# The shift half of a modulation vector: row products on TensorE replaced by ScalarE multiplications and GpSimd sums

## The chip, the cores and the metric

The kernel runs on one core of a Trainium2 chip. The metric is the device time of one execution in microseconds (us), taken as the median of several runs. The profile is of one further execution on the same kind of chip. In its rows PE is TensorE (matrix products; PEld is its weight load), DVE is VectorE, ACT is ScalarE, POOL is GpSimd, and SP is the engine that here only issues DMAs; a q behind an engine's name means its sequencer.

## The reference, cut to what matters

The program is one block of a hybrid encoder (1024 tokens of width 1024): attention, a state-space branch, a merge and a feed-forward part. What matters here is its beginning.

```python
mod = jax.nn.silu(c) @ w_ada[l] + b_ada[l]                 # c: (1, 1024), w_ada: (1024, 6144)
shift1, scale1, gate1, shift2, scale2, gate2 = jnp.split(mod, 6, axis=-1)
h = rms_norm(x, norm1_w[l]) * (1.0 + scale1) + shift1
proj = h @ w_in[l]
```

All values are float32. `shift1` and `scale1` are vectors of 1024 numbers, each the product of one row vector, silu(c), with a 1024 x 1024 block of `w_ada`. Every further step of the program needs `h`.

## The kernel before, in words

`h` is kept transposed: channels on the 128 partitions, tokens along the free axis, in eight channel tiles k of two token halves each. It is kept as the sum of two tiles of a rounded float32 type, `hh` (high part) and `hl` (low part, the rest), and every weight tile is split the same way into `twh` and `twl`. A product of the two is three TensorE products: high by high, low weight by high, high weight by low.

**The modulation** is made in two halves hf of 512 channels. Half 0 gives what channel tiles 0 to 3 need, half 1 what tiles 4 to 7 need. `mod_load(hf, k)` (line 336) brings a 512 KB tile `wada` with 128 rows of `w_ada` (channels k*128 to k*128+127 of c) and two column blocks of 512: block 0 belongs to the shift, block 1 to the scale. Seven such buffers go round (`WADA = 7`). `mod_step(hf, k, wt)` then does two things, for k = 0 to 7:

- scale: DVE multiplies block 1 by silu(c), one number per partition, and adds it to `macc` (lines 345 and 347). After eight steps `macc` holds 128 partial sums per column, one on each partition.
- shift: TensorE multiplies the 128 x 1 column of silu(c) by block 0 and sums over the eight steps into one row of 512 numbers in PSUM, `psr` (line 348).

`mod_scale(hf)` copies that row to SBUF as `srow` (line 356, ACT), and turns `macc` into a column on the partitions: four products of a 128 x 128 piece of `macc` with a vector of ones, which also add up the 128 partitions (line 359). `mod_shift(hf)` turns the row by four products with a single one (line 366), then DVE adds the bias and the norm weight (`modc`, `s`; lines 159 and 368). From then on, `x_high` (line 323, ACT, writes `hh`), `x_full` (line 327, DVE, writes `xf`) and `x_low` (line 159, DVE, `hl` = `xf` - `hh`) can run for the channel tiles of that half.

**The input tokens**: `x_load` brings 128 tokens of x to one of four `xs` buffers, `x_square` sums their squares (line 301, ACT, with a scratch tile `junk`), `x_scale` applies the root mean square, and `x_turn(half, k)` turns channel tile k of four token tiles with four products into one of two PSUM banks `pst` (line 314). For the first token half, tiles 4 to 7 are turned before their modulation is known, and `x_keep` copies them from PSUM to SBUF as `xT` (line 319, ACT), so that the banks and the `xs` buffers come free.

**The first products** of the projection, `first_mm` (line 380, `psq`), run between these steps.

What sets the order: in this whole stage the instructions of SP, DVE, ACT and PE stand in the order in which the program is written (a manual schedule). Each engine takes its own in that order, and waits at each for what it reads. GpSimd has nothing to do in this stage. The names of the tile buffers matter: a tile with `bufs=2` takes over the buffer of the tile before the last of the same `tag`, and its writer waits until that one's readers are done. Behind half 1's eight steps ACT has two weight casts (`twh`, line 173) and DVE the two differences that go with them (`twl`, line 159); then come `mod_scale(1)` and `mod_shift(1)`. The loads of the second half of x wait for the last `x_turn` of the first half, which frees the `xs` buffers.

Of the kernel before, what the change touches and what calls it, by code (L numbers as in the profile page):

```python
# [9 lines left out]
F32 = mybir.dt.float32  # L10
F32R = mybir.dt.float32r
BF16 = mybir.dt.bfloat16
AF = mybir.ActivationFunctionType
ALU = mybir.AluOpType
# [4 lines left out]
P = 128  # L19
S = 1024  # L20
D = 1024
NT = S // P
KT = D // P
# [68 lines left out]
def block(ctx: ExitStack, tc: tile.TileContext, ia, out, upto=99, dbg=None):  # L92
    nc = tc.nc
    V, A, G, T = nc.vector, nc.scalar, nc.gpsimd, nc.tensor
# [41 lines left out]
    ones = cp.tile([P, P], F32, name="ones")  # L136
# [5 lines left out]
    sc = cp.tile([P, 8], F32, name="sc")  # L142
# [15 lines left out]
    def tt(e, o, a, b, op):  # L158
        e.tensor_tensor(out=o, in0=a, in1=b, op=op)  # L159
# [111 lines left out]
    with tc.tile_pool(name="p0", bufs=1) as p0, tc.tile_pool(name="ps0", bufs=1, space=PSUM) as ps0:  # L271
# [8 lines left out]
        ps = ps0.tile([P, 512], F32, name="psv", tag="psv", bufs=2)  # L280
# [16 lines left out]
            dma(xs[t], x_in[t * P:(t + 1) * P, :])  # L297

        def x_square(t):
            junk = p0.tile([P, D], BF16, name="junk", tag="junk", bufs=1)  # L300
            A.activation(junk, xs[t], AF.Square, accum_out=ss[:, t:t + 1])

        def x_scale(t):
# [29 lines left out]
        accs, psrs, pcs = {}, {}, {}  # L333

        def mod_load(hf, k):
            wt = p0.tile([P, 2, 512], F32, name="wada", tag="wada", bufs=WADA)
            dma(wt, w_ada[k * P:(k + 1) * P, 0:2 * D].rearrange("p (a c) -> p a c", a=2)[:, :, hf * 512:(hf + 1) * 512])
            return wt

        def mod_step(hf, k, wt):  # L340

            if k == 0:
                accs[hf] = p0.tile([P, 512], F32, name="macc", tag="macc", bufs=2)
                psrs[hf] = ps0.tile([P, 512], F32, name="psr", tag="psv", bufs=2)
                V.tensor_scalar(out=accs[hf], in0=wt[:, 1], scalar1=sc[:, 0:1], scalar2=None, op0=ALU.mult)
            else:
                V.scalar_tensor_tensor(out=accs[hf], in0=wt[:, 1], scalar=sc[:, k:k + 1], in1=accs[hf], op0=ALU.mult, op1=ALU.add)
            T.matmul(psrs[hf][0:1], sc[:, k:k + 1], wt[:, 0], start=k == 0, stop=k == KT - 1)

        rows_ = {}  # L350

        def mod_scale(hf):

            cs = slice(4 * hf, 4 * hf + 4)
            rows_[hf] = p0.tile([1, 512], F32, name="srow", tag="srow", bufs=1)
            A.copy(rows_[hf], psrs[hf][0:1])
            pcs[hf] = ps0.tile([P, 512], F32, name="psv", tag="psv", bufs=2)
            for j in range(4):
                T.matmul(pcs[hf][:, j:j + 1], accs[hf][:, j * P:(j + 1) * P], ones[:, 0:1], start=True, stop=True)

        def mod_shift(hf):

            cs = slice(4 * hf, 4 * hf + 4)
            ps = pcs[hf]
            for j in range(4):
                T.matmul(ps[:, 4 + j:5 + j], rows_[hf][0:1, j * P:(j + 1) * P], ones[0:1, 0:1], start=True, stop=True)
            tt(V, modc[:, 1, cs], ps[:, 0:4], vecT[:, BA + 8 + 4 * hf:BA + 12 + 4 * hf], ALU.add)
            V.scalar_tensor_tensor(out=s1[:, cs], in0=modc[:, 1, cs], scalar=1.0, in1=vecT[:, N1 + 4 * hf:N1 + 4 * hf + 4],
                                   op0=ALU.add, op1=ALU.mult)
            tt(V, modc[:, 0, cs], ps[:, 4:8], vecT[:, BA + 4 * hf:BA + 4 * hf + 4], ALU.add)  # L370
# [18 lines left out]
        with tc.manual_schedule(engines={mybir.EngineType.SP, mybir.EngineType.DVE, mybir.EngineType.Activation, mybir.EngineType.PE}):  # L389
            for k in range(KT):  # L390
                wt = mod_load(0, k)
                if k < 4:
                    x_load(k)
                    x_square(k)
                mod_step(0, k, wt)
                if k == 3:
                    turn_rows()
                if k == 5:
                    rstd(p0, rs[:, 0:4], ss[:, 0:4], D, 4)
                    x_scale(1)  # L400
                    x_scale(3)
                if k >= 6:
                    x_scale(2 * (k - 6))
            traws = [tw_raw(qkv_srcs(0, kh)) for kh in range(2)]
            mod_scale(0)
            x_turn(0, 0)
            mod_shift(0)
# [48 lines left out]
            mod_shift(1)  # L456
            first_mm(0, 3, (0, 1, 2))
            x_square(4)
            traws = [tw_raw(qkv_srcs(1, kh)) for kh in range(2)]
            for k in range(4, KT):  # L460
# [963 lines left out]
    with tc.tile_pool(name="p5", bufs=1, reuse_waits="tile") as p5, \  # L1424
# [41 lines left out]
        for n, (i, second) in enumerate(jobs):  # L1466
# [13 lines left out]
            for half in range(2):  # L1480
                ps = part[i][half] if i in part else ps5.tile([P, 512], F32, name="psg", tag="psg", bufs=6)
# [39 lines left out]
    with tc.tile_pool(name="p6", bufs=1, reuse_waits="tile") as p6:  # L1521
# [9 lines left out]
        def turned(hf, k):  # L1531
            ps = ps7.tile([P, 512], F32, name="pst", tag="ps1", bufs=4)
            for j in range(4):
                T.transpose(ps[:, j * P:(j + 1) * P], x1[hf * 4 + j][:, k * P:(k + 1) * P], ident)
            return ps
# [4 lines left out]
        for t in range(NT):  # L1540
# [3 lines left out]
            for n in range(2):  # L1544
# [3 lines left out]
                ps = ps7.tile([P, 512], F32, name="pso", tag="ps2", bufs=4)  # L1548
# [12 lines left out]
            if t == 4:  # L1561
                for k in range(KT):
                    ps = turned(0, k)
# [52 lines left out]
        with tc.manual_schedule(engines={mybir.EngineType.PE, mybir.EngineType.DVE, mybir.EngineType.Activation}):  # L1616
# [4 lines left out]
            for j in range(HK):  # L1621
                for q, f in enumerate((fa, fb)):
                    f[j] = tmp("fab")
                    k = q * HK + j
                    ps = ps7.tile([P, 512], F32, name="pst", tag=("ps1", "ps2")[q], bufs=4)
# [278 lines left out]
    with tc.tile_pool(name="p8", bufs=1, reuse_waits="tile") as p8:  # L1904
# [71 lines left out]
        for h in "01":  # L1976
            pss = [banks(first), banks(1 - first)]
            ops = []
            for q in range(2):
                for k in range(KR):  # L1980
                    ops.append((ahead(n), plain_b[q, k]))
                    n += 1
                    j = len(ops) - 1
# [56 lines left out]
```

## Time and profile before

| | |
|---|---|
| time of the kernel, median of 3 runs | 2457.29 us (2456.69 to 2461.17) |
| time of the profiled execution | 2455.24 us |
| its span, first to last instruction | 2453.4 us |
| TensorE busy | 2387.5 us, 97% of the span |
| VectorE busy | 1706.5 us, 70% |
| ScalarE busy | 1092.0 us, 45% |
| GpSimd busy | 829.2 us, 34% |
| mean granted TensorE clock | 0.993 |

The stage that the change touches begins with the span and lies between about 22 and 58 us of it. In a timeline row the first number is the start in us from the beginning of the span, the second the length in us; then come engine, line, operation, the tile written and the tiles read, their shapes, and how many instructions were merged into the row. What stands in square brackets is the idle time of the engine just before, and what ended it. In a row of the chain of waits (the chain of work that ended last) stand start, length, engine, tile and line. In a row of grouped instructions the numbers behind the bar are the busy time in us and the mean length of one in ns, then the idle time before them.

### The profile page before, as it was taken

To read this page: it belongs to the slowest core of one execution; us is meant where nothing else is said; L and a number is where in the kernel's file an instruction comes from. 1 tells how busy PE (TensorE), PEld (TensorE's weight loads), DVE (VectorE), ACT (ScalarE), POOL (GpSimd) and SP (SyncE) were. 2 spreads that over 40 slices of the span, in tenths; PEclk is the share of its full clock that TensorE was granted. 3 is DMA by queue.
4 is the path that set the end of the run, shared out by engine and by line. 5 is a ranking of instruction groups with operands and counts; after the bars stand their busy time and mean duration, and the time that the engine had idled before them with its cause. 6 is when DMAs were issued, how large, how long until landed. Compare 5 with 4: busy or idle time off the path is not lost.

```text
span 2453.4 us, 32245 instructions
## 1 busy us (share of the span) xinstructions
PE 2387.5 (97%) x11307; PEld 1900.2 (77%) x11307; DVE 1706.5 (70%) x2325; ACT 1092.0 (45%) x1884; POOL 829.2 (34%) x637
## 2 busy tenths in 40 slices
PE   8999999999989999999989999999999999999999
PEld 4998877888867777777767767787787888788887
DVE  5876435777756666666577796558568887767794
ACT  5455413555566666666333343354242222364430
POOL 0221107666611111110356665534006885023200
PEclk9999999999999999999999999999999999999999
DMA  7664751333531212111667765486325554654422
GB/s 257 185 184 139 255 170 65 95 103 111 183 114 52 91 52 80 57 53 48 223 207 222 223 209 177 142 282 202 125 86 193 196 174 159 231 172 142 153 79 83
DMA packets 288596, 366.53 MB, mean 149 GB/s; under 512 B 33962, under 2 KB 168850, under 8 KB 288434
## 3 DMA queue, kind: packets, MB, share of 16 engines
q1 hardware_dynamic: 216246, 288.77, 36.9%
q10 hardware_dynamic: 72187, 75.70, 9.1%
q8 instruction: 90, 1.47, 0.2%
q14 instruction: 73, 0.59, 0.1%
HBM read 250.54 MB, written 113.84 MB: 149 GB/s over the span
## 4 chain that ended last, share of the span: by engine, by line
PE 84%; DVE 7%; DMA 3%; issue 2%; ACT 2%; POOL 0%; ACTq 0%; SPq 0%; DVEq 0%; POOLq 0%
PE pst L1053 5%; PE psg L211 4%; PE psg L213 4%; PE psg L212 4%; PE pp L1503 4%; PE pp L1505 4%; PE pp L1504 4%; PE p L1919 3%; PE p L1918 3%; PE p L1917 3%; PE psc L916 3%; PE psc L917 3%; PE psc L918 3%; PE psq L518 3%; PE psq L519 3%; PE psq L517 3%
## 5 line engine op out<-in xcount | busy, mean ns | idle before, releaser
L1040 DVE TENSOR_REDUCE nm<-pss 128x1 f32<-128x1024 f32 x128 | 156.7, 1225 | 125.2 <-PE pss L1038 122.8
L1042 ACT ACTIVATE pf<-pss,nm 128x1024 f32<-128x1024 f32 x128 | 142.8, 1116 | 98.9 <-PE pst L1053 96.3
L159 DVE TENSOR_TENSOR pl<-pst,ph 128x512 fp32r<-128x512 f32 x256 | 167.6, 683 | 27.1 <-ACT ph L173 27.0
L1053 PEld LDWEIGHTS pst<-masks,pf 128*128 128x128 f32 x1024 | 117.5, 140 | 73.3 <-issue 33.3
L517 PE MATMUL psq<-twh,hh 128*128 128x512 f32 (+1 forms) x448 | 168.3, 380 | 3.0 <-ACT twh L173 3.0
L518 PE MATMUL psq<-twl,hh 128*128 128x512 f32 (+1 forms) x448 | 169.3, 379 | 0.9 <-DVE twl L159 0.9
L173 ACT CAST ph<-pst 128x512 fp32r<-128x512 f32 x256 | 145.7, 585 | 54.9 <-PE pst L1053 38.2
L1053 PE MATMUL pst<-masks,pf 128*128 128x128 f32 x1024 | 157.3, 276 | 13.0 <-DVE pl L159 10.6
L519 PE MATMUL psq<-twh,hl 128*128 128x512 f32 (+1 forms) x448 | 168.6, 377 | 0.0
L159 POOL TENSOR_TENSOR av<-av,rz 64x512 f32<-64x512 f32 x32 | 41.9, 1310 | 348.1 <-issue 99.3
L1917 PE MATMUL p<-o,o 128*128 128x512 f32 x400 | 153.6, 390 | 3.0 <-ACT o L173 1.6
L1918 PE MATMUL p<-o,o 128*128 128x512 f32 x400 | 155.2, 389 | 0.2 <-DVE o L159 0.2
L1919 PE MATMUL p<-o,o 128*128 128x512 f32 x400 | 153.7, 389 | 0.0
L173 ACT CAST wop<-ws 128x512 fp32r<-128x512 f32 x116 | 71.8, 621 | 124.4 <-PE pp L1505 78.7
L862 DVE SCALAR_TENSOR_TENSOR tap<-pad,cwT,tap 128x1024 f32<-128x1024 f32 x96 | 123.4, 1285 | 5.2 <-ACT tap L860 3.8
L159 POOL TENSOR_TENSOR ws<-r,r 128x512 f32<-128x512 f32 x29 | 41.4, 1428 | 220.3 <-DMA r<-in_w_mlp_dram 168.9
L159 POOL TENSOR_TENSOR sl<-sl 128x512 f32<-128x512 f32 x32 | 49.4, 1546 | 179.5 <-DVE o L159 72.4
L173 ACT CAST o<-sl 128x512 fp32r<-128x512 f32 x92 | 56.9, 623 | 104.6 <-PE p L1919 88.7
L1091 PE MATMUL pv<-pl,v 128*64 128x512 f32 x256 | 102.1, 419 | 0.0
L159 DVE TENSOR_TENSOR o<-sl,o 128x512 fp32r<-128x512 f32 x92 | 72.7, 793 | 41.3 <-ACT o L173 41.3
L211 PE MATMUL psg<-hh,whi 128*128 128x512 f32 x224 | 95.7, 427 | 1.2 <-ACT ost L1002 1.2
L517 PEld LDWEIGHTS psq<-twh,hh 128*128 128x128 f32 x448 | 84.5, 189 | 15.0 <-ACT twh L173 3.4
(457 smaller groups left out, 7035.6 us busy)
## 6 DMA issues: line engine op xcount, KB each, us to landing
ar<-r SPq DMA_DIRECT2D x100, 256.0 KB
wada<-in_w_ada_dram SPq DMA_DIRECT2D x48, 512.0 KB
r<-in_w_mlp_dram SPq DMA_DIRECT2D x32, 512.0 KB
sl<-in_w_mlp_dram SPq DMA_DIRECT2D x64, 256.0 KB
r<-in_w_in_dram SPq DMA_DIRECT2D x26, 512.0 KB
r<-ro ACTq DMA_DIRECT2D x49, 256.0 KB
r<-as SPq DMA_DIRECT2D x48, 256.0 KB
xb<-cst ACTq DMA_DIRECT2D x20, 512.0 KB
```

Of the source, the lines that this page charges most:

```text
L159: e.tensor_tensor(out=o, in0=a, in1=b, op=op)
L173: (e_hi or A.copy)(hi, src)
L211: T.matmul(ps, hi[:, k], ahi[k][half], start=k == 0, stop=False)
L517: T.matmul(o, hhi[k][half][:, sl], hi[:, k % 2, :n], start=k == 0, stop=False)
L518: T.matmul(o, hhi[k][half][:, sl], lo[:, k % 2, :n], start=False, stop=False)
L519: T.matmul(o, hlo[k][half][:, sl], hi[:, k % 2, :n], start=False, stop=k == KT - 1)
L1040: V.tensor_reduce(out=nm, in_=ps, axis=AX.X, op=ALU.max, negate=True)
L1042: A.activation(pfs[u], ps, AF.Exp, bias=nm, accum_out=zall[:, u:u + 1])
L1053: T.transpose(pt[:, k], pf[:, (hf * 4 + k) * P:(hf * 4 + k + 1) * P], ident)
L1917: T.matmul(ps, a[:, 0, sl], b[0], start=start, stop=False)
L1918: T.matmul(ps, a[:, 0, sl], b[1], start=False, stop=False)
L1919: T.matmul(ps, a[:, 1, sl], b[0], start=False, stop=stop)
```

## The change

Only half 1 changes. Its shift is made in the way in which the scale is: ACT multiplies block 0 of `wada` by silu(c) (a `Copy` with a scale per partition) into a 128 x 512 tile `sacc`, and GpSimd adds the eight products up, seven sums in all. The result holds 128 partial sums per column, and `mod_shift(1)` turns it and adds up the partitions by four products with the full vector of ones. The eight row products of half 1 (`psr`, line 348), the copy of its row (`srow`) and the four products with a single one are gone. Half 0 stays as it is.

The first product (k = 0) takes a third `macc` buffer and is the tile into which GpSimd adds. The others take the two buffers of the tag `junk`, which had one buffer and is also the scratch tile of `x_square`. So product k + 2 on ACT waits for the sum k on GpSimd, and the first two of `x_square`'s later tiles wait for the last two sums.

```diff
         def x_square(t):
-            junk = p0.tile([P, D], BF16, name="junk", tag="junk", bufs=1)
+            junk = p0.tile([P, D], BF16, name="junk", tag="junk", bufs=2)
             A.activation(junk, xs[t], AF.Square, accum_out=ss[:, t:t + 1])
...
             if k == 0:
-                accs[hf] = p0.tile([P, 512], F32, name="macc", tag="macc", bufs=2)
-                psrs[hf] = ps0.tile([P, 512], F32, name="psr", tag="psv", bufs=2)
+                accs[hf] = p0.tile([P, 512], F32, name="macc", tag="macc", bufs=3)
                 V.tensor_scalar(out=accs[hf], in0=wt[:, 1], scalar1=sc[:, 0:1], scalar2=None, op0=ALU.mult)
             else:
                 V.scalar_tensor_tensor(out=accs[hf], in0=wt[:, 1], scalar=sc[:, k:k + 1], in1=accs[hf], op0=ALU.mult, op1=ALU.add)
-            T.matmul(psrs[hf][0:1], sc[:, k:k + 1], wt[:, 0], start=k == 0, stop=k == KT - 1)
+            if hf:
+                t = p0.tile([P, 512], F32, name="sacc", tag="macc" if k == 0 else "junk", bufs=3 if k == 0 else 2)
+                A.activation(t, wt[:, 0], AF.Copy, scale=sc[:, k:k + 1])
+                if k == 0:
+                    accs[2] = t
+                else:
+                    tt(G, accs[2], accs[2], t, ALU.add)
+            if hf == 0:
+                if k == 0:
+                    psrs[hf] = ps0.tile([P, 512], F32, name="psr", tag="psv", bufs=2)
+                T.matmul(psrs[hf][0:1], sc[:, k:k + 1], wt[:, 0], start=k == 0, stop=k == KT - 1)
...
-            rows_[hf] = p0.tile([1, 512], F32, name="srow", tag="srow", bufs=1)
-            A.copy(rows_[hf], psrs[hf][0:1])
+            if hf == 0:
+                rows_[hf] = p0.tile([1, 512], F32, name="srow", tag="srow", bufs=1)
+                A.copy(rows_[hf], psrs[hf][0:1])
...
             for j in range(4):
-                T.matmul(ps[:, 4 + j:5 + j], rows_[hf][0:1, j * P:(j + 1) * P], ones[0:1, 0:1], start=True, stop=True)
+                js = slice(j * P, (j + 1) * P)
+                if hf == 0:
+                    T.matmul(ps[:, 4 + j:5 + j], rows_[hf][0:1, js], ones[0:1, 0:1], start=True, stop=True)
+                else:
+                    T.matmul(ps[:, 4 + j:5 + j], accs[2][:, js], ones[:, 0:1], start=True, stop=True)
```

On TensorE, the place from the turning of tiles 3 and 4 of x to the turning of half 1's `macc` stands like this before:

```order
L314 MATMUL pst<-masks,xs 128x128 x8
L348 MATMUL psr<-wada,sc 1x512
L380 MATMUL psq<-twh,hh_0_348 128x400 x4
L348 MATMUL psr<-wada,sc 1x512
L314 MATMUL pst<-masks,xs 128x128 x8
L348 MATMUL psr<-wada,sc 1x512
L314 MATMUL pst<-masks,xs 128x128 x4
L348 MATMUL psr<-wada,sc 1x512
L359 MATMUL psv<-ones,macc 128x1 x4
```

and like this with the change, where the last product reads `macc`, which DVE makes:

```order
L314 MATMUL pst<-masks,xs 128x128 x8
L394 MATMUL psq<-twh,hh_0_348 128x400 x4
L314 MATMUL pst<-masks,xs 128x128 x12
L369 MATMUL psv<-ones,macc 128x1 x4
L394 MATMUL psq<-twl,hh_0_348 128x400
```

The four row products of this piece, and the four ahead of it, are gone; nothing else changed its place. On ACT, the same stretch, from the high parts `hh` of tiles 0 to 3 of the first half (numbers 344 to 350) to the casts, before:

```order
L323 ACTIVATE hh_0_344<-pst,modc,s_334 128x512
L323 ACTIVATE hh_0_346<-pst,modc,s_334 128x512
L323 ACTIVATE hh_0_348<-pst,modc,s_334 128x512
L173 CAST twh<-traw 128x2x400
L323 ACTIVATE hh_0_350<-pst,modc,s_334 128x512
L319 COPY xT<-pst 128x512 x4
L173 CAST twh<-traw 128x2x400 x2
L356 COPY srow<-psr 1x512
```

and with the change:

```order
L323 ACTIVATE hh_0_344<-pst,modc,s_334 128x512
L349 ACTIVATE sacc<-wada,sc 128x512
L323 ACTIVATE hh_0_346<-pst,modc,s_334 128x512
L349 ACTIVATE sacc<-wada,sc 128x512 x2
L323 ACTIVATE hh_0_348<-pst,modc,s_334 128x512
L173 CAST twh<-traw 128x2x400
L349 ACTIVATE sacc<-wada,sc 128x512 x2
L323 ACTIVATE hh_0_350<-pst,modc,s_334 128x512
L319 COPY xT<-pst 128x512
L349 ACTIVATE sacc<-wada,sc 128x512
L319 COPY xT<-pst 128x512 x2
L349 ACTIVATE sacc<-wada,sc 128x512
```

The eight products stand between the high parts and the copies of x; the last one (not shown) stands behind the fourth copy and ahead of the two casts. On DVE and SP no instruction is added, removed or moved. GpSimd gets the seven sums as its first work. Outside this stage the order is the same on every engine, but for one product of the later projection by `w_o`, which stands two places further back.

## The prediction

> **What bounds the kernel now.** I read first the page's shares of the chain of waits, then the busy times of the stretch that the change touches, then the chain through that stretch. The page's chain:
>
> ```profile
> PE 84%; DVE 7%; DMA 3%; issue 2%; ACT 2%; POOL 0%; ACTq 0%; SPq 0%; DVEq 0%; POOLq 0%
> ```
>
> TensorE sets the end, so time taken off its order early comes off the end, unless another engine is late there. The stretch from 26 to 48 us (length; busy us of PE, PEld, DVE, ACT and POOL, each with its count; clock; DMA share; GB/s):
>
> ```profile
> 26.00:48.00 22.00, 21.64 (x100) 12.83 (x101) 15.53 (x24) 9.80 (x16) 0.00 (x0) 1.00 0.80 273
> ```
>
> PE is busy 21.64 of 22 us, GpSimd not at all, ACT 9.80. DVE, at 15.53, is second. The chain through it:
>
> ```profile
> 28.38 0.95 PE psr L348 x2
> ...
> 42.17 0.95 PE psr L348 x2
> 43.12 0.98 PE psv L359 x8
> 44.10 1.57 PE psq L380 x8
> 45.68 0.99 PE psv L366 x8
> 46.67 0.02 issue
> 46.70 0.17 DVE modc L159
> ```
>
> Seven row products of 0.95 us lie on it (the first and the last are shown, each two records), then the turning of `macc`, eight first products, the turning of the row, and at 46.70 `modc`, for which the high parts of tiles 4 to 7 wait. Behind that the chain is ACT's:
>
> ```profile
> 55.15 2.20 ACT xs L306 x2
> 57.35 0.04 issue
> 57.39 0.33 PE pst L314
> ```
>
> ACT alternates high parts and squares from 47.22 on, and PE waits for its result at 57.39. A later `modc` is therefore a later 57.39 by as much, and from there PE works through to the end. I count everything at `modc`.
>
> **The change part by part.** *Removed on PE.* The first of the eight row products frees nothing:
>
> ```profile
> 26.11 1.02 PE L348 MATMUL psr<-wada,sc 128*1 128x512 f32 x2 [0.40 <-DMA wada<-in_w_ada_dram]
> 27.38 1.01 PE L380 MATMUL psq<-twh,hh 128*128 128x400 f32 x4 [0.24 <-ACT hh L323]
> ```
>
> PE waits for `hh` until 27.38 after it. The other seven give 7 x 0.95 = 6.65 us, so PE could reach the turning of `macc` at 43.12 - 6.65 = 36.5. The four products that turn the shift are as many as before (0.98 by the `macc` row, 0.99 by the other): nothing.
>
> *What is late next: DVE.* That turning needs the last `macc`. DVE's whole order there:
>
> ```profile
> 28.36 0.81 DVE L327 TENSOR_SCALAR xf<-pst,s,modc 128x512 f32<-128x512 f32 x1
> 29.20 0.69 DVE L159 TENSOR_TENSOR hl<-xf,hh 128x512 fp32r<-128x512 f32 x1
> 29.81 1.53 DVE L347 SCALAR_TENSOR_TENSOR macc<-wada,sc,macc 128x512 f32<-128x512 f32 x2
> 32.28 0.81 DVE L327 TENSOR_SCALAR xf<-pst,s,modc 128x512 f32<-128x512 f32 x1 [0.94 <-ACT hh L323]
> 33.02 0.99 DVE L159 TENSOR_TENSOR twl<-traw,twh 128x800 fp32r<-128x800 f32 x1
> 33.93 0.68 DVE L159 TENSOR_TENSOR hl<-xf,hh 128x512 fp32r<-128x512 f32 x1
> 34.53 1.53 DVE L347 SCALAR_TENSOR_TENSOR macc<-wada,sc,macc 128x512 f32<-128x512 f32 x2
> 37.20 0.81 DVE L327 TENSOR_SCALAR xf<-pst,s,modc 128x512 f32<-128x512 f32 x1 [1.14 <-ACT hh L323]
> 38.05 0.69 DVE L159 TENSOR_TENSOR hl<-xf,hh 128x512 fp32r<-128x512 f32 x1
> 38.66 2.32 DVE L347 SCALAR_TENSOR_TENSOR macc<-wada,sc,macc 128x512 f32<-128x512 f32 x3
> 43.58 1.89 DVE L159 TENSOR_TENSOR twl<-traw,twh 128x800 fp32r<-128x800 f32 x2 [2.61 <-ACT twh L173]
> ```
>
> The last `macc` ends at 38.66 + 2.32 = 40.98. Of that 0.94 and 1.14 us are idle, waits for `hh` and thereby for PE's turning of x; with PE early they go. DVE then ends at 38.9, and the gain is 43.12 - 38.9 = 4.2 us, not 6.65, if DVE's instructions keep their length.
>
> *Added on GpSimd: seven sums, and what they do to DVE.* The only stretch nearby in which both work:
>
> ```profile
> 95.37 0.18 DVE L159 TENSOR_TENSOR qrs<-qrs,rs_t 128x20 f32<-128x20 f32 x1
> ...
> 99.73 2.38 DVE L159 TENSOR_TENSOR qrs<-qrs,rs_t 128x20 f32<-128x20 f32 x1
> ```
>
> ```profile
> 99.65 2.43 POOL L159 TENSOR_TENSOR qn<-qn,tab 128x1024 f32<-128x1024 f32 x1 [14.37 <-DVE t L159]
> ```
>
> The same tiny DVE instruction takes 0.18 us, and 2.38 when a GpSimd instruction started 0.08 us ahead of it: it ends with that one. With both queues full, near the end of the program:
>
> ```profile
> 2000.39 1.75 POOL L159 TENSOR_TENSOR ws<-ws,r 128x512 f32<-128x512 f32 x1
> 2002.09 1.75 POOL L159 TENSOR_TENSOR as<-ro,as 128x512 f32<-128x512 f32 x1
> ```
>
> ```profile
> 2000.90 0.68 DVE L159 TENSOR_TENSOR ro<-c,pp 128x512 f32<-128x512 f32 x1
> 2001.50 1.19 DVE L159 TENSOR_TENSOR wop<-ws,wop 128x512 fp32r<-128x512 f32 x1
> 2002.61 1.78 DVE L1683 SCALAR_TENSOR_TENSOR ro<-ro 128x512 f32<-128x512 f32 x1
> ```
>
> They take turns. GpSimd ends at 2002.14, DVE at 2002.69, GpSimd at 2003.84, DVE at 2004.39: a sum holds DVE up for 2003.84 - 2002.69 = 1.15 us, and DVE's instruction then needs 0.55. The DVE row at 2000.90, with an operand in PSUM (`pp`), is not delayed. In our stretch `hl`, `macc` and `twl` read two SBUF tiles each, `xf` reads PSUM.
>
> The Trainium skill, page "SBUF — State Buffer", section "SBUF: two separate sides", says that VectorE instructions with two SBUF inputs and GpSimd instructions contend for one port pair, and that whoever starts first keeps it for its whole instruction. By that the gain above is eaten sum by sum, as here; were the port merely shared between overlapping rows, a sum would cost DVE less than its length and part of the gain would stay. The row at 99.73, held up to the end of the other, agrees with the page.
>
> The price of a sum alone, bounded by two groups:
>
> ```profile
> L159 POOL TENSOR_TENSOR pad<-pad,p 128x512 f32<-128x512 f32 x26 | 28.3, 1110 | 27.7 <-ACT p L956 22.0 <-ACT wop L173 5.7
> L159 POOL TENSOR_TENSOR df<-df 128x512 f32<-128x512 f32 x4 | 5.5, 1372 | 0.2
> ```
>
> Between 1.11 and 1.37 us; I take the 1.15 of the turn-taking, since a contended sum is what is paid here.
>
> Sums 1 to 5 are ready before the last `macc`: their products stand on ACT ahead of, or right behind, the first copy of x. Sums 6 and 7 are not: their products stand behind copies whose bank waits for the last `xf` from PSUM, which DVE reaches only after five `macc`. So DVE is held up 5 x 1.15 = 5.75 us, less one `xf` of 0.81 that runs beside a sum: 38.9 + 5.75 - 0.81 = 43.84 for the last `macc`. Behind it DVE still has the two `twl`, at 0.98, against sums 6 and 7: 43.84 + 2 x 1.15 + 2 x 0.98 = 48.1 for `modc`. A DVE instruction that was held up needs 0.55 instead of some 0.70 afterwards, seven times: 47.1 at the earliest. PE's own order gives 43.84 + 0.98 + 1.57 + 0.99 = 47.4, inside that. I take the middle, 47.6, which is 0.9 later than 46.70.
>
> *Added on ACT: eight multiplications, minus one copy.*
>
> ```profile
> 36.39 0.78 ACT L323 ACTIVATE hh<-pst,modc,s 128x512 fp32r<-128x512 f32 x1 [3.40 <-PE pst L314]
> 37.07 0.57 ACT L319 COPY xT<-pst 128x512 f32<-128x512 f32 x1
> ```
>
> A copy of that shape takes 0.57, so 8 x 0.57 = 4.6 us on an engine idle for 12 of 22 us, with idle pieces like the 3.40 shown; between 0.57 and 0.78 each it is hidden. What is not free is the ring of two product buffers: product 4 waits for sum 2, and `hh` of tile 3 and the copies stand behind it. Sum 2 ends near 33, ahead of 36.39, where that `hh` stands now; hidden too, while sums start on time.
>
> *DMA.* The loads of x wait for the last turning of x:
>
> ```profile
> 41.88 0.34 SPq L297 DMA_DIRECT2D xs<-in_x_dram  x1
> ```
>
> ```profile
> 45.39 1.06 ACT L301 ACTIVATE junk<-xs 128x1024 bf16<-128x1024 f32 x1 [0.61 <-DMA xs<-in_x_dram]
> ```
>
> From issue to first use it takes 3.5 us. With the last `xf` near 41 that turning lies near 42.5 (one turning, one copy, one turning, 0.5 to 0.6 each), so x lands at 46, before `hh` of tile 4 at 48. `wada` loads keep their release, DVE's first step of half 1, so they neither gain nor lose.
>
> *Sum.* +0.9 us on the profiled execution's 2455.24: 2456.1. Its time lies 2.05 under the median of the runs shown, 2457.29; against that median the forecast is 2457.29 + 0.9 = 2458.2. The case's own range is 2456.9 (DVE gives way less, -0.4) to 2460.0 (sums at 1.37: 7 x 0.22 = 1.5 more, and 0.3 on ACT).
>
> **The rivals.**
>
> *The sums hide.* DVE is not held up, or gets its turns where it would idle; DVE's order binds at 38.9 and 4.2 us are won: 2457.29 - 4.2 = 2453.1. For it: GpSimd has no work here, and DVE's 15.53 of 22 us leave room. Against it: DVE's two waits are the room that the 4.2 us already spend, and the rows at 99.73 and 2002.61 show whole delays.
>
> *The sums become the end: slower.* `mod_shift` waits for sum 7, and sum 1 does not run at its first chance. If GpSimd takes its turns at 1.75 us from request to end (row 2002.09) and ACT's ring then holds back `hh` of tile 3, the last `xf` and with it the last copies move by about 2 us beyond my 41; products 6 and 7, sums 6 and 7 and both `twl` follow, and `modc` comes near 50: 2457.29 + 3.4 = 2460.7. It decides once sum 2 ends after 36. For it: ACT's own order stands behind the ring, and x's second half with it. Against: sum 1 is ready at 29.2, when DVE has only begun. A first instruction on GpSimd that is slow to begin would do the same:
>
> ```profile
> 79.25 1.55 POOL L159 TENSOR_TENSOR tab<-rope,qkw 128x512 f32<-128x512 f32 x1 [78.81 <-DMA qkw<-in_k_norm_w_dram]
> ```
>
> It took 1.55, so 0.3 more than a later one at most. The Trainium skill's "GPSIMD Engine Reference", section "Instruction dispatch", puts about 6 us on the first call of a freshly loaded kernel, without a row of its own; by that the first sum would start near 35 and this rival would hold, at an estimated 2461. This trace cannot show whether that lies in the wait ahead of 79.25.
>
> *That the change does not do what it says* can be left out: its order shows the products gone and the sums in place.
>
> **How the numbers follow.** The turn-taking forecast gets 0.70, hidden sums 0.13, sums as the end 0.17. The predicted time is 2458.2. About 0.2%, 4.9 us, is what a measurement of this kernel can tell from no change: faster is below 2452.4, slower above 2462.2. No case reaches either on its own; the runs before, 4.5 us apart, could carry half of the hidden-sums case below (0.07), and of the slow case and what I overlook above (0.09), which leaves 0.84. The range reaches from 2453.5, near the hidden sums, to 2461.5, past the slow case.
>
> **What would show it right or wrong.** Right: seven GpSimd records between 29 and 47 us, most near 1.7 rather than 1.1; `macc` and `hl` records of 1.2 to 1.8 instead of 0.75 and 0.69; idle PE of several us ahead of the turning of `macc`, put down to DVE; `modc` between 46.3 and 49. Wrong: `macc` at 0.75 throughout and `modc` near 42.5 (hidden sums); a first sum after 33, ACT idle behind GpSimd ahead of `hh` of tile 3, or PE waiting for sum 7 (sums as the end). Wrong altogether: a difference of `modc` that does not come back at 57.39 or at the end.

## The result, and the profile after

The changed kernel takes 2464.93 us (median of 13 runs, 2461.14 to 2468.12) where the kernel before takes 2457.98 in the same series (13 runs, 2454.05 to 2461.17): a ratio of 1.0029, 95% interval 1.0020 to 1.0037, or 7 us slower (4.9 to 9.1). Forecast was 2458.2, within 2453.5 to 2461.5.

The stretch from 26 to 48 us of the profile after, in the columns that the prediction explains:

```profile
26.00:48.00 22.00, 13.96 (x64) 12.45 (x65) 21.05 (x20) 13.46 (x21) 10.76 (x7) 0.78 0.76 261
```

PE is busy 13.96 us instead of 21.64, so its products are gone. DVE is busy 21.05 instead of 15.53 and has become the full engine; GpSimd's seven sums are there. The granted clock, the share of its full speed that TensorE was given, has fallen from 1.00 to 0.78 on the mean. Now the chain of waits through the stretch, after:

```profile
37.78 1.68 DVE macc L346
...
44.05 0.76 DVE macc L346
44.81 0.04 issue
44.86 1.86 PE psv L369 x8
46.72 2.88 PE psq L394 x8
49.60 1.50 PE psv L380 x8
51.10 12.00 PE psq L394 x54
```

The seven row products are replaced by DVE's `macc`, as forecast, with the last one at 44.81. But the three PE rows behind it take 1.86, 2.88 and 1.50 us where the same work took 0.98, 1.57 and 0.99 before. And from 51.10 the chain is PE's for 12 us, up to the turning of x at 63.09, where it was ACT's before, up to the same turning at 57.39. The reason stands in PE's timeline and in the table of stretches, both after:

```profile
36.98 0.66 PE L314 MATMUL pst<-masks,xs 128*128 128x128 f32 x4 [0.68 <-ACT xT L319]
41.90 1.11 PE L314 MATMUL pst<-masks,xs 128*128 128x128 f32 x4 [4.27 <-DVE xf L327]
44.86 1.86 PE L369 MATMUL psv<-ones,macc 128*128 128x1 f32 x8 [1.85 <-DVE macc L346]
...
54.77 0.54 PE L394 MATMUL psq<-twh,hl 128*128 128x400 f32 x1
...
55.41 0.35 PE L394 MATMUL psq<-twl,hh 128*128 128x400 f32 x1
```

```profile
38.00:42.00 4.00, 0.10 (x1) 0.11 (x2) 3.93 (x4) 0.87 (x2) 2.46 (x2) 0.97 0.27 62
42.00:46.00 4.00, 2.15 (x10) 1.75 (x10) 3.70 (x5) 2.71 (x4) 1.54 (x1) 0.50 0.65 207
46.00:50.00 4.00, 4.00 (x16) 3.97 (x15) 1.69 (x2) 1.16 (x2) 0.00 (x0) 0.50 0.97 373
50.00:54.00 4.00, 4.00 (x15) 3.98 (x15) 2.10 (x6) 2.40 (x4) 0.00 (x0) 0.50 0.88 219
54.00:56.00 2.00, 2.00 (x9) 1.99 (x9) 1.21 (x3) 2.00 (x5) 0.00 (x0) 0.66 0.01 1
```

PE waits 4.27 and 1.85 us for DVE. At the end of the long wait the granted clock drops to 0.50, and it stays there until about 55 us, although PE is fully busy from 44.86 on. A product of 400 columns takes 0.54 us in that time and 0.35 behind it. (An earlier stretch of low clock, 0.79 on the mean from 26 to 34 us, also lies behind a wait, of 1.65 us for `hh`; DVE's rows below show no wait behind it up to the last `macc`.)

DVE and GpSimd after, the rows that answer to those of the prediction:

```profile
29.29 1.64 DVE L159 TENSOR_TENSOR hl<-xf,hh 128x512 fp32r<-128x512 f32 x1
30.85 2.55 DVE L346 SCALAR_TENSOR_TENSOR macc<-wada,sc,macc 128x512 f32<-128x512 f32 x2
33.32 0.80 DVE L327 TENSOR_SCALAR xf<-pst,s,modc 128x512 f32<-128x512 f32 x1
34.04 2.07 DVE L159 TENSOR_TENSOR twl<-traw,twh 128x800 fp32r<-128x800 f32 x1
36.03 1.75 DVE L159 TENSOR_TENSOR hl<-xf,hh 128x512 fp32r<-128x512 f32 x1
37.71 3.41 DVE L346 SCALAR_TENSOR_TENSOR macc<-wada,sc,macc 128x512 f32<-128x512 f32 x2
...
42.49 2.32 DVE L346 SCALAR_TENSOR_TENSOR macc<-wada,sc,macc 128x512 f32<-128x512 f32 x3
45.03 2.65 DVE L159 TENSOR_TENSOR twl<-traw,twh 128x800 fp32r<-128x800 f32 x2 [0.23 <-ACT twh L173]
51.13 0.16 DVE L159 TENSOR_TENSOR modc<-psv,vecT 128x4 f32<-128x4 f32 x1 [3.44 <-PE psv L380]
```

```profile
29.10 2.97 POOL L159 TENSOR_TENSOR sacc<-sacc 128x512 f32<-128x512 f32 x2 [28.66 <-ACT sacc L349]
33.98 6.59 POOL L159 TENSOR_TENSOR sacc<-sacc 128x512 f32<-128x512 f32 x4 [1.92 <-ACT sacc L349]
44.40 1.54 POOL L159 TENSOR_TENSOR sacc<-sacc 128x512 f32<-128x512 f32 x1 [3.82 <-ACT sacc L349]
```

`hl` takes 1.64 and 1.75 instead of 0.69, `twl` 2.07 instead of 0.99, two `macc` 2.55 and 3.41 instead of 1.53. `xf`, which reads PSUM, stays at 0.80. The three `macc` from 42.49 on, with GpSimd idle until 44.40, take 2.32 for three as before.

### The profile page after: what moved, and what is told of

Same layout as the page of the kernel before. It is cut to its first block, busy times and chain, and to the rows that moved or that the text cites. A ratio compares the mean times of both kernels' runs of the same rounds, so it can differ in the third digit from the quotient of the medians.

```text
span 2463.9 us, 32236 instructions
## 1 busy us (share of the span) xinstructions
PE 2384.3 (97%) x11291; PEld 1905.0 (77%) x11291; DVE 1718.7 (70%) x2325; ACT 1097.0 (45%) x1891; POOL 837.5 (34%) x644
## 4 chain that ended last, share of the span: by engine, by line
PE 79%; DVE 8%; DMA 7%; ACT 3%; issue 3%; POOL 1%; SPq 0%; ACTq 0%; DVEq 0%; POOLq 0%
PE pst L1067 5%; PE psg L211 4%; PE psg L213 4%; PE psg L212 4%; PE pp L1517 3%; PE pp L1519 3%; PE pp L1518 3%; PE p L1933 3%; PE p L1932 3%; PE p L1931 3%; PE psc L930 3%; PE psc L931 3%; PE psc L932 3%; PE psq L532 3%; PE psq L533 3%; PE psq L531 3%
```

## The experiments

Theory A: two prices are paid. The sums hold VectorE up, and TensorE's wait for VectorE costs it its clock. Rival B: the clock is a by-product and costs nothing; the hold-up alone explains the loss. Rival C: the clock is the whole loss; the hold-up costs nothing. Rival D: VectorE is late by the waits among ACT, GpSimd and the ring of two buffers, not by what it reads. Rival E: the loss is chance of the profiled execution. Two edits separate the prices of A: the sums of `macc` in PSUM (no hold-up of `macc`), and TensorE kept busy (clock).

**1. TensorE kept busy.** `warm(n)` issues n products of 128 x 400 that nobody reads (its definition is not shown).

```diff
+            warm(20)
             x_turn(0, 7)
...
+            warm(8)
             mod_scale(1)
```

> The change, with 28 extra products on TensorE whose result nobody reads: 20 (3.7 us at 0.183 each) ahead of the last turning of x, where it sat idle for 4.27 us, and 8 (1.5 us) ahead of the turning of macc, where it sat idle for 1.85. Nothing else moves. Theory A (the sums hold VectorE up, TensorE then idles, and its granted clock falls to 0.50 and stays there for 13 us): VectorE's records stay as with the change, the last macc still ends near 44.8, the granted clock stays at 1.00 after 42 us, modc comes at 44.86 + 0.98 + 1.57 + 0.99 = 48.4 instead of 51.13, and some 3 to 4 us of the 7 come back: near 2461. Rival B (the late last macc alone makes the loss; the clock is a record without a price): no faster than the change, 2465. Rival C (the whole loss is the clock): back to the kernel before or below, 2458 or less.

Measured: ratio 1.0013 (1.0004 to 1.0022). VectorE is late as before, the last `macc` ends at 44.33. TensorE's timeline and the stretches:

```profile
38.62 3.92 PE L393 MATMUL warm<-twh,hh 128*128 128x400 f32 x20
...
42.74 1.72 PE L393 MATMUL warm<-twh,hh 128*128 128x400 f32 x8
44.39 1.05 PE L369 MATMUL psv<-ones,macc 128*128 128x1 f32 x8
...
46.85 0.95 PE L380 MATMUL psv<-ones,sacc 128*128 128x1 f32 x8
```

```profile
38.00:42.00 4.00, 3.79 (x22) 3.79 (x23) 3.93 (x4) 1.37 (x3) 2.95 (x3) 1.00 0.11 19
42.00:46.00 4.00, 4.00 (x27) 3.68 (x27) 3.26 (x5) 2.71 (x4) 1.28 (x1) 1.00 0.55 175
```

The clock stays at 1.00, the turnings take 1.05 and 0.95, and `modc` stands at 47.84 instead of 51.13. Work that computes nothing takes 3.3 us off `modc`, and the loss in the median goes from 0.29% to 0.13%: B is out. C is out as well, since VectorE is as late as before and the time stays above the kernel before.

**2. The sums of `macc` in PSUM.** VectorE then has one SBUF input in `macc`.

```diff
-                accs[hf] = p0.tile([P, 512], F32, name="macc", tag="macc", bufs=3)
+                if hf:
+                    accs[hf] = ps0.tile([P, 512], F32, name="pacc", tag="psv", bufs=2)
+                else:
+                    accs[hf] = p0.tile([P, 512], F32, name="macc", tag="macc", bufs=3)
...
+                o = accs[hf]
+                if hf and k == KT - 1:
+                    o = p0.tile([P, 512], F32, name="macc", tag="macc", bufs=3)
...
```

> The change, with half 1's macc accumulated in PSUM by VectorE for the steps 0 to 6, and written to SBUF in step 7 alone. So macc's instructions read one SBUF tile and one PSUM tile; GpSimd's seven sums stay. Theory A: macc's records fall back to about 0.75 beside running sums, only hl and twl are still held up (four instructions by up to 1.15 us ahead of the last macc), which ends between 39.5 and 42 instead of 44.8; TensorE's waits shrink under 4 us, and the time lies between 2454 and 2460, below the change. Rival D (VectorE is late because of the waits among ACT, GpSimd and the ring of two buffers, not because of what it reads): the last macc stays near 44.8 and the time at 2465.

Measured: ratio 1.0019 (1.0010 to 1.0028). VectorE's rows, then the turning of `macc` on TensorE:

```profile
29.31 1.64 DVE L159 TENSOR_TENSOR hl<-xf,hh 128x512 fp32r<-128x512 f32 x1
30.87 1.54 DVE L352 SCALAR_TENSOR_TENSOR pacc<-wada,sc,pacc 128x512 f32<-128x512 f32 x2
```

```profile
41.24 1.87 PE L376 MATMUL psv<-ones,macc 128*128 128x1 f32 x8 [2.43 <-DVE macc L352]
```

Beside the sum that takes `hl` to 1.64, two `macc` take 1.54, as without sums; the last ends at 41.19. The last step, which writes to SBUF but reads `pacc` from PSUM, takes 0.75 beside a running sum as well, so it is the two SBUF inputs that are held up, and D is out. The time missed the expectation (2454 to 2460; the median is 2463.64), because the clock fell all the same: TensorE, now waiting 2.43 us for `macc`, needs 1.87 for the turning, and `modc` is at 47.52.

**3. Fills in place of sums.** GpSimd only writes; half 1's shift holds only its first product.

```diff
-                    tt(G, accs[2], accs[2], t, ALU.add)
+                    G.memset(t, 0.0)
+                    G.memset(t, 0.0)
```

> The change, with each sum on GpSimd replaced by two fills with zeros of the product's buffer (about 0.55 us each by the fill of 128x1024 in 1.08 us): GpSimd is as busy and the ring of two buffers waits for it as before, but it reads nothing. The shift of half 1 is then silu(c) times the first tile of w_ada alone, so that part of the computation is left out. Theory A: VectorE's records are 0.75 for macc and 0.69 for hl throughout, the last macc ends near 39, modc near 42.6, and the time is some 4 us below the kernel before: 2454. Rival D (waits among queues and the ring): close to the change, 2465. If writing holds VectorE up as well: macc records above 1 us again, and the time between the two.

Measured: ratio 1.0003 (0.9994 to 1.0012). GpSimd and VectorE:

```profile
30.36 0.52 POOL L353 MEMSET sacc<- 128x512 f32 x1
```

```profile
30.12 1.53 DVE L346 SCALAR_TENSOR_TENSOR macc<-wada,sc,macc 128x512 f32<-128x512 f32 x2
...
45.78 0.16 DVE L159 TENSOR_TENSOR modc<-psv,vecT 128x4 f32<-128x4 f32 x1 [2.35 <-PE psv L381]
```

Fills beside `macc` hold nothing up; the sums, which also read SBUF, do. The Trainium skill, page "SBUF — State Buffer", section "SBUF: two separate sides", has a VectorE instruction with two SBUF inputs locked out only by a GpSimd instruction that reads SBUF, and these rows agree. `macc` ends at 40.76 (expected near 39; a stretch of low clock from 25.3 to 32.1 had delayed what it waits for), yet `modc` only at 45.78: the clock is at 0.54 from 42 to 46, behind a wait of 1.97 us. So the time missed the expected 2454 as well (median 2459.91).

**4. The changed kernel again.**

> The changed kernel once more, for a second profile: the steps behind 64 us. In the first pair of profiles the difference is 5.5 us at 64 us and 10.3 to 10.6 from 1720 us on, while the medians differ by 7.0. If the steps at 305, 1210 and 1720 us come from the change they stand at the same places again; if they come from the moment at which the clock falls in waits that both kernels have, they are elsewhere, or of other size, while the 5.5 us at 64 us and modc near 51 stay.

Measured: 2464.3 us. The waits are 4.28 and 1.85 us, the clock 0.50 from 42 to 54, `modc` at 50.97. The picture repeats; E does not hold for it. The steps behind the stage: counted from the first profile before, TensorE's instructions of the first profile after are 5.5 us late at 64 us, 5.4 at 1150, 7.4 at 1250 and 10.3 at 1750; those of this one 4.9, 6.4, 7.3 and 10.2.

**5 and 6. Both cures together**: experiment 2, and experiment 3, each with `warm` products.

```diff
+            warm(10, True)     # ahead of first_mm(0, 0, (0,))
...
+            warm(4)            # ahead of x_turn(0, 7)
...
+            warm(10)           # ahead of mod_scale(1); 8 in experiment 6
```

(The places are given as comments; `warm(10, True)` issues ten unread turnings of x.)

> The change with both suspects taken away: half 1's macc in PSUM as in the run before, and unread products on TensorE in its waits (10 turnings of x ahead of the first product of tile 0, 4 products ahead of the last turning of x, 10 ahead of the turning of macc). Theory A (the sums hold VectorE up, and the idle TensorE loses its clock, two prices that add): VectorE as with macc in PSUM, the last macc near 41.0, the granted clock 1.00 from 26 to 58 us, modc at 41.0 + 0.98 + 1.57 + 0.99 = 44.6, so 2.1 ahead of the 46.70 of the kernel before, and 2 us below that kernel's time: a gain of 0.05 to 0.12%. Rival C (the clock is the whole loss, the held-up VectorE costs nothing): no better than the run with unread products and macc in SBUF, 3 us above the kernel before. Rival B (the clock has no price): no better than macc in PSUM without them, 4.5 us above.

> The fills in place of the sums (the shift of half 1 left out but for its first product, as in the run before), with unread products on TensorE: 10 turnings ahead of the first product, 4 ahead of the last turning of x, 8 ahead of the turning of macc. GpSimd then reads nothing, and TensorE stays busy. Theory A: VectorE's records of 0.75 and 0.69, its two waits for hh gone, the last macc between 39 and 39.5, granted clock 1.00, modc near 43, and about 4 us below the kernel before: 2455, the gain that the sum without turn-taking gave. If the row products' place was not worth 4 us at all: as the run with fills alone, level with the kernel before.

Measured: ratios 1.0002 (0.9993 to 1.0011) and 0.9997 (0.9988 to 1.0005). `modc` of the two, one after the other:

```profile
45.08 0.16 DVE L159 TENSOR_TENSOR modc<-psv,vecT 128x4 f32<-128x4 f32 x1 [1.48 <-PE psv L387]
```

```profile
43.45 0.16 DVE L159 TENSOR_TENSOR modc<-psv,vecT 128x4 f32<-128x4 f32 x1 [0.76 <-PE psv L381]
```

In the stage both cures work, and nearly add: experiments 1 and 2 alone take 3.2 and 3.5 us off the changed kernel's `modc`, experiment 5 takes 6.0. The clock is 1.00 from 34 us on. Of the 4.2 us of room that the prediction found ahead of VectorE, experiment 6 has 3.25 against the 46.70 that the prediction started from, and 4.45 against the mean of all profiles before (experiment 11). At the end neither is told from the kernel before, where 2 and 4 us less were expected: both expectations missed.

**7. The kernel before again.**

> The kernel before once more, for a second profile. Every profile taken since lies 3 to 5 us further behind the first one of the kernel before at its end than at 64 us, in steps near 300, 1220 and 1720 us. If these steps are the first profile's luck with the clock in waits that all kernels share, this one has them as well and is 2 to 4 us longer than 2453.4. If the change makes them, it agrees with the first to 1 us at 1150, 1300 and 1800 us.

Measured: 2460.6 us. It has a stretch of low clock of its own, 0.57 from 26 to 30 us, that the first profile lacks; its `modc`:

```profile
47.76 0.16 DVE L159 TENSOR_TENSOR modc<-psv,vecT 128x4 f32<-128x4 f32 x1 [1.22 <-PE psv L366]
```

Its span is 2458.8 us, 5.4 longer than the first (2 to 4 were expected). Counted as in experiment 4 it is 1.1 us late at 64 us, 2.3 at 1150, 1.7 at 1250 and 6.5 at 1750. So the late step, between 1250 and 1750 us, comes without the change as well, and that near 1215 is missing here. E holds in part, for the kernel before: the profile that the prediction stood on was an early one. Experiments 10 and 11 follow this up.

**8 and 9. The program's own products as filler**: 8 on experiment 2, 9 on the changed kernel.

```diff
+            first_mm(0, 2, (1,))
             x_turn(0, 7)
...
+            first_mm(0, 2, (2,))
+            first_mm(0, 3, (0,))
             mod_scale(1)
-            first_mm(0, 2, (1, 2))
             mod_shift(1)
-            first_mm(0, 3, (0, 1, 2))
+            first_mm(0, 3, (1, 2))
```

> Half 1's macc accumulates in PSUM for steps 0 to 6 as in the kernel with the PSUM sums alone, and TensorE's waits are filled with products of the program's own instead of unread ones: the second third of channel tile 2's first products (4) stands ahead of the last turning of x, its last third and the first third of tile 3 (8) ahead of the turning of macc; nothing stands between the turnings of macc and of the GpSimd sum. Nothing is left out or added. Theory A (VectorE's hold-up plus TensorE's clock): the last macc ends at 41.2 to 41.7, the wait ahead of its turning is under 1 us, the granted clock stays near 1.00 from 38 us on, and with 0.98 and 0.99 for the two turnings modc stands at 43.2 to 44.2, against 46.70 before: 2.5 to 3.5 us won, a median ratio near 0.9987. Rival (only unread filler at the very end holds the clock; the moved products are missing behind modc): waits of over 1 us remain ahead of macc or appear behind modc, the clock falls to 0.5 there, and the ratio is 1.000 or above.

> The changed kernel with only the order of TensorE's first products moved as in the run beside it (4 ahead of the last turning of x, 8 ahead of the turning of macc); macc stays in SBUF. Nothing is left out. Theory A: VectorE is held up as in the changed kernel, last macc at 44.5 to 44.8; the wait ahead of the last turning of x falls from 4.27 to 3.5, that ahead of the turning of macc from 1.85 to 0 to 0.5. The long wait still takes the clock to 0.5, and the two turnings take 1.86 and 1.70: modc near 48.5, against 51.13, since eight products no longer stand between them; the median is about 2 to 3 us under the changed kernel's, near 1.002. Rival (clock plays no part, the order alone was at fault): the two turnings take 0.98 and 0.99 and modc stands at 46.8.

Measured: ratios 1.0000 (0.9992 to 1.0009) and 1.0021 (1.0011 to 1.0031). TensorE in experiment 8, then in 9, then VectorE in 9:

```profile
41.34 1.05 PE L376 MATMUL psv<-ones,macc 128*128 128x1 f32 x8 [0.99 <-DVE macc L352]
42.25 1.03 PE L387 MATMUL psv<-ones,sacc 128*128 128x1 f32 x8
```

```profile
42.50 1.12 PE L314 MATMUL pst<-masks,xs 128*128 128x128 f32 x4 [3.55 <-DVE xf L327]
45.74 0.95 PE L369 MATMUL psv<-ones,macc 128*128 128x1 f32 x8
```

```profile
45.64 2.66 DVE L159 TENSOR_TENSOR twl<-traw,twh 128x800 fp32r<-128x800 f32 x2 [0.23 <-ACT twh L173]
48.22 0.15 DVE L159 TENSOR_TENSOR modc<-psv,vecT 128x4 f32<-128x4 f32 x1
```

In 8 the stage went as A expected, with `modc` at 43.40, but the median did not follow (expected near 0.9987); the profiled execution, at 2454.80 us, was the fastest of the eleven, whose median is 2457.89. In 9 a wait of 3.55 us still took the clock down (0.59 from 42 to 46), but it came back before the turning; `modc`, at 48.22, stands near A's 48.5, but not by A's path. The last `macc` ended 0.7 us later than A said, the two turnings took 0.95 and 1.05 instead of 1.86 and 1.70, and were done near 47.6; `modc` then came right behind VectorE's two `twl`, which the seventh sum held up to 2.66 us (1.89 before). So the agreement is luck. The rival in the expectation (the order alone was at fault) had the short turnings, but `modc` at 46.8; with VectorE late, this run does not decide between the two. Experiment 1 does: there the order is that of the changed kernel, and the clock alone moves `modc` by 3.2. And a wait's length alone does not say how long the clock stays down.

**10 and 11. The kernel before once more, and with the change's buffer counts alone** (`junk` 2, `macc` 3; no instruction differs).

> The kernel before, once more, for the spread of its own profile. The first two profiles have modc at 46.70 and 47.76; the second has a stretch of granted clock 0.5 to 0.67 from 26 to 30 us, behind waits of 0.16 to 0.33 us, that the first does not have. If that stretch is chance, this one has modc at one of the two, between 46.6 and 47.9, and its end between 2453 and 2459; if the changed kernel's loss were of that kind too, it would be as large as this one's shift against the first.

> The kernel before with only the buffer counts of the change (a second buffer of the tag junk, a third of macc); no instruction is changed. It asks whether the place of the later tiles in memory costs time: the runs of all changed kernels so far end some 3 us later than their stage up to 64 us accounts for. If placement costs it: 2 to 4 us slower, ratio 1.0008 to 1.0016, with modc where it was, at 46.7 to 47.9. If not: ratio 1.000, within 0.0009, and the shares of the stages as before.

Measured: 10 took 2457.29 us with `modc` at 47.90; 11 has the ratio 1.0000 (0.9991 to 1.0009), so the place of the later tiles does not cost the 2 to 4 us that were to be tested, nor more than 2.2. The stretch from 26 to 30 us, in experiment 10 and in 11:

```profile
26.00:30.00 4.00, 3.93 (x8) 1.34 (x8) 3.96 (x7) 1.45 (x2) 0.00 (x0) 0.57 1.02 376
```

```profile
26.00:30.00 4.00, 3.90 (x7) 1.34 (x8) 3.96 (x7) 1.45 (x2) 0.00 (x0) 0.50 1.02 366
```

Four profiles of the same instructions have `modc` at 46.70, 47.76, 47.90 and, in experiment 11, 49.17 (outside the expected 46.7 to 47.9), and only the first has no low clock at 26 us. Their mean is 47.9.

**12. No row products, and nothing in their place**, with the products moved as in 8.

```diff
-            T.matmul(psrs[hf][0:1], sc[:, k:k + 1], wt[:, 0], start=k == 0, stop=k == KT - 1)
+            if hf == 0 or k == 0:
+                T.matmul(psrs[hf][0:1], sc[:, k:k + 1], wt[:, 0], start=k == 0, stop=hf == 1 or k == KT - 1)
```

> The kernel before without the row products of steps 1 to 7 of half 1, and without ScalarE products, GpSimd sums or more buffers: the shift of half 1 holds only its first product, so it is not the reference's. TensorE's first products are moved ahead as in the run with moved products (4 ahead of the last turning of x, 8 ahead of that of macc), to keep its clock. It asks what 6.65 us less on TensorE are worth at the end if nothing takes their place. VectorE binds: last macc at 39 to 40, modc at 41.5 to 43, 4 to 6 us ahead of the kernel before. If what is won at modc reaches the end: 4 to 5 us faster, ratio 0.9980 to 0.9985. If later waits take it back whoever wins it: ratio 0.9995 to 1.0005, and the loss in the PSUM run with moved products is not the change's own.

Measured: ratio 0.9998 (0.9989 to 1.0007), the second of the two outcomes. `modc` is won, the end is not:

```profile
43.26 0.16 DVE L159 TENSOR_TENSOR modc<-psv,vecT 128x4 f32<-128x4 f32 x1 [0.63 <-PE psv L367]
```

It stands 0.3 us behind the expected 41.5 to 43, since the turning of the row waited 1.07 us for `srow`. This kernel has neither sums nor ScalarE products, and does not end early either; just behind `modc` its clock falls as well (0.63 from 42 to 46).

**The runs together** (`modc` from one profile each; for the rows with two or four, all of them):

| kernel | last `macc` ends | `modc` | ratio to before (95%) |
|---|---|---|---|
| before | 40.98 to 43.45 | 46.70, 47.76, 47.90, 49.17 | 1 |
| changed | 44.81, 44.64 | 51.13, 50.97 | 1.0029 (1.0020 to 1.0037) |
| 1: TensorE busy | 44.33 | 47.84 | 1.0013 (1.0004 to 1.0022) |
| 2: `macc` in PSUM | 41.19 | 47.52 | 1.0019 (1.0010 to 1.0028) |
| 5: both | 41.58 | 45.08 | 1.0002 (0.9993 to 1.0011) |
| 3: fills | 40.76 | 45.78 | 1.0003 (0.9994 to 1.0012) |
| 6: fills, TensorE busy | 39.96 | 43.45 | 0.9997 (0.9988 to 1.0005) |
| 8: PSUM, products moved | 41.28 | 43.40 | 1.0000 (0.9992 to 1.0009) |
| 9: products moved | 45.41 | 48.22 | 1.0021 (1.0011 to 1.0031) |
| 12: no row products | 39.95 | 43.26 | 0.9998 (0.9989 to 1.0007) |

Each ratio is against runs of the kernel before in the same series. Up to `modc` the difference can be split, each step between two kernels. From the kernel before (47.9 on the mean) to experiment 6: 4.45 us won, by TensorE's relief. From there to experiment 1: 4.4 lost, by the sums. From there to the changed kernel (51.05 on the mean of two): 3.2 lost, by the clock (0.4 of it in a last `macc` that ends later). No version beats both kernels by more than can be told from nothing.

**What stays open** is the rest of the way. `modc` is 3.2 us later than the mean before, and TensorE's instructions near 64 us, matched one by one between the profiles, are 4.0 us later (5.5 and 4.9 against 0 to 2.5, counted from the first profile before). The median is 7 later. Experiments 8 and 12 are 4.5 and 4.6 us early at `modc`, and their medians are not early. So the medians of the kernels without the row products lose 2 to 5 us more than the profiles at 64 us account for. The profiles themselves show little of it: from there to the end they take 2456.1 us on the mean in four of the kernel before (2453.4 to 2459.1), and 2457.3 in ten without the row products (2455.4 to 2461.4). And a profiled execution is one of its series, up to 3.3 us faster than the median (experiment 2) or 5.2 slower (experiment 11). One piece could be located, near 1215 us. TensorE's waits there, before, and then in experiment 12:

```profile
1217.43 1.12 PE L1220 MATMUL pst<-xdb,xbb 128*128 128x512 f32 x2 [1.28 <-POOL xdb L159]
```

```profile
1213.62 1.13 PE L1223 MATMUL pst<-xdb,xbb 128*128 128x512 f32 x2 [0.76 <-POOL xdb L159]
1218.47 1.12 PE L1223 MATMUL pst<-xdb,xbb 128*128 128x512 f32 x2 [1.66 <-POOL xdb L159]
```

Between 1150 and 1250 us the ten profiles of kernels without the row products fall back by 0.8 to 2.3 us (counted as above), eight of them with a second wait like this one (0.2 to 1.7 us); the four with row products by -0.8 to 0.9, all with one wait. Why, the runs do not say, since nothing was changed there; the stretch ahead of it and the one behind showed no such difference beyond the scatter, which is several us between profiles of one kernel.

## Why the prediction was wrong, point by point

**Right: what binds.** TensorE's relief ends at DVE, and DVE and the sums take turns. *The size of a turn*: 1.15 us a sum was forecast. Up to the last `macc` the held-up rows are longer by 0.95 + 1.02 + 1.08 + 1.07 + 1.88 = 6.00 us, and six sums lie beside them: 1.0 each. DVE's two waits for `hh` are gone, as forecast, and its own path, 48.1 in the prediction, is done at 47.68 (45.03 + 2.65).

**Off by one sum: the last `macc`.** Forecast 43.84, measured 44.81. The prediction counted five sums ahead of it and put the sixth behind the last `xf`. GpSimd's second row shows four more sums running through to 40.57, six in all: product 6 stands on ACT behind the copy of tile 6, and the turning of that tile waited for an earlier copy (the 0.68 <-ACT `xT` of PE's row at 36.98), not for the last `xf`. Only the turning of tile 7 does (the 4.27). With the sixth, the prediction's own sum gives 43.84 + 1.15 = 44.99.

**The step that failed: "PE's own order gives 43.84 + 0.98 + 1.57 + 0.99 = 47.4".** The three durations were read from a PE that had not waited. The prediction itself named, among the signs, several us of idle PE ahead of that turning, and put what they do to PE's clock at nothing. In their place stand 1.86 + 2.88 + 1.50 = 6.24 us, 2.70 more; with the 0.97 of the last `macc` that is the whole distance from 47.4 to 51.13 but 0.06. Experiment 1 gives the clock back and has 47.84, near the forecast 47.6, with the last `macc` at 44.33.

Behind `modc` the half clock goes on to 55 us, and so another step falls: the chain does not pass to ACT at `modc`, because PE has its 54 products still to do, those up to 55 us at the low clock (12.00 us in all). The turning of x that stood at 57.39 comes at 63.09, so 5.7 us later, not the 4.4 of `modc`. "I count everything at `modc`" left that out. At 64 us these steps account for 4.0 of the 7 us, from mean to mean; the rest stays open, as said above.

The Trainium skill, page "TensorE: Matmul & The Clock Gate", section "Part 1: The HAM clock gate (the "warmup" mystery)", says that an idle window of about 3.4 us takes the clock to one half, and about 3.4 us of sustained work brings it back. The first half agrees with the 4.27 us here, but the clock fell with waits of 2.43 us in experiment 2 and 1.97 in experiment 3 too, so one wait need not be that long. By the second half, an estimate from the page's figure, the clock would have been back near 48.3 (44.86 + 3.4); it came back near 55, after 10 us of full work. In both the measurement decides.

**Right: the sums do not become the end.** Sum 7 ends at 45.94, ahead of the products that read it at 49.40. No first sum was slow: it starts at 29.10, as its product ends. *ACT is hidden*: eight products at 0.72 each, inside the bounds 0.57 to 0.78; the ring delayed no `hh` (tile 3's stands at 34.36, ahead of 36.39 before). *The x loads*: issued at 42.40 instead of 41.88, with a wait of 0.30 us on ACT and no more.

**The base.** 46.70 was the earliest of four. Measured from the mean, 47.9, the same 47.6 is 0.3 us less instead of 0.9 more. The step "carries to the end" stays unproven either way: experiments 8 and 12 show gains of 4.5 us at `modc` whose medians do not show them, and the intervals leave room for 2.0 and 2.7 of these.

## What to carry to other kernels

Before work is taken off TensorE, ask what it does in the gap: a wait of a few us can halve its clock, and then what follows the wait is to be costed longer until the clock is back, here 1.5 to 1.9 times its length (the rows of 1.86, 2.88 and 1.50). Where the waits were made short and filled with products that are due anyway (experiment 8), the clock held. And a GpSimd instruction that reads SBUF beside VectorE's two-input instructions costs VectorE most of its own length, here 1.0 us of a sum that takes 1.28 where it starts first (experiment 1, at 44.37): put one operand in PSUM, or don't place them side by side.

## What was unexpected of the hardware

- The clock's return takes very different times: after the waits of 4.27 and 1.85 us it stayed at 0.50 through 10 us of full work; in experiment 9, after 3.55 us, it was back within 4 us. But the times are not arbitrary. Here is the whole stretch at 0.50 in the changed kernel, and in experiment 9:

```profile
41.74:55.37 13.63, 11.63 (x41) 11.16 (x42) 8.86 (x15) 7.63 (x13) 1.54 (x1) 0.50 0.73 234
```

```profile
41.90:45.29 3.39, 2.79 (x10) 2.78 (x11) 3.29 (x5) 1.64 (x3) 0.29 (x1) 0.50 0.35 91
```

In the clock records of all fourteen traces, every stretch at 0.50 that ends within the program lasts 3.41 us or two, three or four times that: 13.65 in both profiles of the changed kernel, 10.24 in experiment 2, 6.83 in 3, 3.41 in 9 and 12. The kernel before fits this: no such stretch early on in the first profile, 3.41 us in experiments 7 and 10, 6.83 in 11, and `modc` later by 1.1, 1.2 and 2.5 us. What decides how many there are, no run shows.
- The clock can fall without a long wait: in experiments 10 and 11 it was at 0.57 and 0.50 from 26 to 30 us, while PE was busy 3.9 of 4 us there and had waited for a load of `wada` by only 0.58 and 0.44 us just ahead (0.40 in the first profile, whose clock stayed up). The same instructions therefore reach `modc` anywhere from 46.70 to 49.17.
- A GpSimd fill of 0.52 us beside VectorE costs it nothing, one sum 1.0 us.
